# A diffusion-transformer layer on one core: everything up to LayerNorm 1 in an order from a list scheduler

## The chip, the core and the metric

The kernel runs on one core of a Trainium2 chip. Five engines work side by side, each through its own instructions in order: TensorE (PE: matmuls, and PEld its weight loads), VectorE (DVE), ScalarE (ACT), GpSimd (POOL) and SyncE (SP), which issues the DMAs of this kernel. [...] The metric is the device time of one execution in microseconds, as the median of several runs; less is better.

## The reference

One layer of a diffusion transformer in fp32: 256 latent tokens `x` and 256 context tokens `ctx`, width 2048, FFN width 5632. Cut to what matters here (the context only supplies keys and values, since there is one layer):

```python
sh1, sc1, g1, sh2, sc2, g2 = split(silu(c) @ w_ada + b_ada, 6)       # w_ada: 2048 x 12288
csh1, csc1 = the first two of split(silu(c_ctx) @ w_ada + b_ada, 6)
h  = (x   * (1 + sc1)  + sh1)  @ w_in                                # w_in: 2048 x 3072
hc = (ctx * (1 + csc1) + csh1) @ w_in
# 8 heads A: window of 128, rotary, sink logit;  8 heads B: global, q and k RMS-normalised, rotary
# each group: 2 key/value heads; latent queries see latent keys and all context keys in one softmax
heads = concat(attend_A(h, hc), attend_B(h, hc))
x = layer_norm(2**0.25 * x + g1 * (heads @ w_out))                   # LayerNorm 1; w_out: 2048 x 2048
u = x * (1 + sc2) + sh2
x = layer_norm(2**0.25 * x + g2 * ((silu(u @ w_gate) * (u @ w_up)) @ w_down))
```

## The kernel before, in words

*Products.* A product with a large weight is made to fp32 accuracy from three fast ones. A weight piece of 128 x 1024 is split into `hi` (a ScalarE copy, L121) and `lo` (VectorE: raw minus hi, L122), the tokens likewise, and `mm3` (L131 to L133) adds hi·hi, lo·hi and hi·lo in a PSUM bank. A weight load (`load_raw`, L101) brings up to 1 MB, that is four k-tiles of 512 columns, into one of six raw buffers: four in the pool `wraw` and two in `araw`, taken in the turn main, main, araw (`ring`).

*Modulation.* The columns of sh1 and sc1, for tokens and context, are sums over `w_ada` that TensorE makes in four groups of 32 columns (`ada_steps`, L230); ScalarE copies them (L237), and a small selection matmul turns them into columns (L253). g1, g2 and most of sh2 and sc2 are summed on VectorE instead (L204).

*Stages up to LayerNorm 1.* The input projection goes over groups of 1, 1, 2, 4 and 8 k-tiles (`GROUPS`). For each group `prep` makes the columns of the modulation, transposes `x` and `ctx` (L351), modulates (L355) and splits them (L357, L358); then `in_part` multiplies them with six blocks of 512 columns of `w_in` for two or four row tiles, and VectorE adds every result to its sum in SBUF (L390, L392). With the last group the attention begins: rotary and transposes of keys and queries (L435 to L461, L477), scores (four matmul lines on `wk` banks), a maximum (L499), an exponential (L507), a weighing by the inverse sum (L517), a transpose (L525), two copies into `pT` (L527), and the values (L537) for four heads at once. The output projection (`out_block`) is cut into pieces that fit between; its sums end in the residual and the statistics of LayerNorm 1 (L665 to L670, L629 to L646).

*PSUM.* Four banks `acc` for the products, three `wk` for all short work, one for the modulation's sums.

*Order.* Steps are merged by hand (`merge` spreads lists evenly over each other), and the framework's own scheduler fits instructions within that, except in the first products and around LayerNorm 1, which run as written (`manual_schedule`, L716 and L753). SP issues DMAs in the order that results, and a load waits until its raw buffer is free. Warm-up matmuls on the identity (`warm`, L707) keep TensorE busy where it would wait: 28, then 2 and 10 around the first selection, 4 before the first products, and 8 and 6 at LayerNorm 1.

*After LayerNorm 1* come gate and up (L796 on), down (L894 on) and LayerNorm 2.

Of the kernel before, what the change touches and what calls it, by code (L numbers as in the profile page):

```python
# [45 lines left out]
LAG_S = 2  # L46


@with_exitstack
def dit_layer(ctx: ExitStack, tc: tile.TileContext, x, c, cx, c_ctx, w_ada, b_ada, w_in, q_norm_g,  # L50
# [10 lines left out]
    wk_ps = ctx.enter_context(tc.tile_pool(name="wk_ps", bufs=3, space=PSUM))  # L61
# [6 lines left out]

    ada_ps = ctx.enter_context(tc.tile_pool(name="ada_ps", bufs=1, space=PSUM))
# [20 lines left out]

    ring = [wraw, wraw]
    turn = [0]

    def raw_tile():
        turn[0] += 1
        return ring[turn[0] % len(ring)].tile([P, G4 * NB], F32, tag="raw", name="raw")
# [38 lines left out]
    def rsqrt(pool, v, n, eng):  # L135
        y = pool.tile([P, n], F32, tag=f"rs_y{n}", name="rs_y", bufs=2)
        t = pool.tile([P, n], F32, tag=f"rs_t{n}", name="rs_t", bufs=2)
        nc.vector.tensor_single_scalar(t.bitcast(I32), v.bitcast(I32), 1, op=ALU.logical_shift_right)
        nc.vector.tensor_scalar(y.bitcast(I32), t.bitcast(I32), -1.0, float(0x5F3759DF), op0=ALU.mult, op1=ALU.add)
        for _ in range(3):  # L140
            eng.scalar_tensor_tensor(t, y, -0.5, y, op0=ALU.mult, op1=ALU.mult)
            eng.tensor_mul(t, t, v)
            eng.scalar_tensor_tensor(y, t, 1.5, y, op0=ALU.add, op1=ALU.mult)
        return y
# [3 lines left out]
    ring.append(ea.enter_context(tc.tile_pool(name="araw", bufs=ADA_BUFS)))  # L148
# [30 lines left out]
    def ada_vector_steps(starts, width, sums, done):  # L179


        st = {}
        ns = len(starts)
        w = ns * width
        nk = G4 * NB // w

        def step(g):
            if g == 0:
                st["a"] = sums()
                nc.gpsimd.memset(st["a"], 0.0)  # L190
                for i, c0 in enumerate(starts):
                    nc.sync.dma_start(st["a"][0:1, i * width : (i + 1) * width], b_ada[0:1, c0 : c0 + width])
            a = st["a"]
            raw = raw_tile()
            rv = raw.rearrange("p (k i n) -> p i k n", k=nk, i=ns)
            for i, c0 in enumerate(starts):
                nc.sync.dma_start(
                    rv[:, i],
                    w_ada[g * nk * P : (g + 1) * nk * P, c0 : c0 + width].rearrange("(k p) n -> p k n", p=P),
                )  # L200
            piece = min(w, 2 * NB)
            for j in range(nk):
                for c in range(0, w, piece):
                    nc.vector.scalar_tensor_tensor(a[:, c : c + piece], raw[:, j * w + c : j * w + c + piece],  # L204
                                                   cs[:, g * nk + j, 2:3], a[:, c : c + piece],
                                                   op0=ALU.mult, op1=ALU.add)
            if g == KD // nk - 1:
                done(a)

        return [lambda g=g: step(g) for g in range(KD // nk)]  # L210

# [3 lines left out]
    def ada_steps(starts, width, done, copy_tile=None):  # L215


        st = {}
        nk = G4 * NB // width
        ns = KD // nk  # L220
        nb = len(starts)

        def step(i, g):
            raw = load_raw(w_ada, g * nk, nk, starts[i], width)
            if i == 0 and g == 0:
                st["ps"] = ada_ps.tile([P, NB], F32, tag="ada", name="adaps")
            for c in range(nk):
                k = g * nk + c
                j = k % 4
                nc.tensor.matmul(  # L230
                    st["ps"][32 * j : 32 * j + 32, :width], lhsT=cs[:, k, 2 - 2 * i : 34 - 2 * i],
                    rhs=raw[:, c * width : (c + 1) * width],
                    start=(i == 0 and k < 4), stop=(i == nb - 1 and k >= KD - 4),
                )
            if i == nb - 1 and g == ns - 1:
                sb = copy_tile() if copy_tile else pa.tile([P, NB], F32, tag="t2k", name="ada", bufs=5)
                nc.scalar.copy(sb[:, :width], st["ps"][:, :width])  # L237
                done(sb)

        return [lambda i=i, g=g: step(i, g) for i in range(nb) for g in range(ns)]  # L240

    def ada_pair(c0, ncol, shift, scale, copy_tile=None, later=None):

        def done(sb):
            if later is None:
                columns(sb)
            else:
                later.append(lambda: columns(sb))

        def columns(sb):  # L250
            ps = wk_bank()
            for j in range(ncol):
                nc.tensor.matmul(ps[:, 4 * j : 4 * j + 4], lhsT=sb[:, j * P : (j + 1) * P], rhs=sel, start=True, stop=True)  # L253
            pv = ps[:, 0 : 4 * ncol].rearrange("p (j i s) -> p j i s", i=2, s=2)
            bs, bc = (bcol[:, k : k + ncol, None].to_broadcast([P, ncol, 2]) for k in (c0 // P, c0 // P + KD))
            nc.vector.tensor_tensor(shift, pv[:, :, 0, :], bs, op=ALU.add)
            nc.vector.scalar_tensor_tensor(scale, pv[:, :, 1, :], 1.0, bc, op0=ALU.add, op1=ALU.add)

        return ada_steps((c0, c0 + D), ncol * P, done, copy_tile)

    def ada_rows(c0, dst, sums):

        width = dst.shape[-1]

        def done(sb):
            for s in range(0, width, NB):
                ps = wk_bank()
                nc.tensor.matmul(ps, lhsT=ones, rhs=sb[:, s : s + NB], start=True, stop=True)  # L268
                nc.scalar.copy(dst[:, s : s + NB], ps)

        return ada_vector_steps((c0,), width, sums, done)
# [18 lines left out]
    def consts():  # L290
# [4 lines left out]
        nc.sync.dma_start(sinkb, sink_logit[0:1, :].to_broadcast([P, 8]))  # L295
        nc.gpsimd.tensor_scalar_mul(nsink, sinkb, -1.0)
        nc.vector.tensor_copy(identb, ident)
# [18 lines left out]

    qacc = [[pa.tile([P, NB], F32, tag=f"q{gi}{t}", name="qacc") for t in range(NT)] for gi in range(4)]
    u, rms, kT = {}, {}, {}
# [3 lines left out]


    kvacc = [[b4([P, 2, NB], F32, "kvacc") for _ in range(2)] for _ in range(2)]

    def prep(g):

        k0, n = GROUPS[g]
        return sum((prep_part(g, k, min(n, G4)) for k in range(k0, k0 + n, G4)), [])

    def prep_part(g, k0, n):

        st = {}

        def loads():
            nc.sync.dma_start(xt[:, :, k0 * P : (k0 + n) * P],
                              x[:, k0 * P : (k0 + n) * P].rearrange("(t p) d -> p t d", p=P))
# [640 lines left out]
```

## Time and profile before

| | us |
|---|---|
| median of 3 runs | 1190.5 (1188.59 to 1191.16) |
| the profiled execution | 1189.62 |
| its span, first to last instruction | 1187.8 |
| TensorE busy | 1158.3 (98%) |
| VectorE busy | 800.4 (67%) |
| ScalarE busy | 530.3 (45%) |
| bytes moved | 292.93 MB, mean 247 GB/s |

The page of the profile gives busy time for each engine, the granted TensorE clock (PEclk) and the DMA share in slices, the chain of waits that ended last, and groups of equal instructions with their count, busy time, mean duration, and the idle time ahead of them with what ended it. A stretch of the span can be asked for by itself (windows), and the instructions of a stretch in order of time (timeline). Matmuls are pipelined and their ends are modelled: one of 512 columns lasts 0.39 us in a row, while the next starts earlier, so starts are read here rather than durations. A fp32 matmul that is not split stands as two rows. LayerNorm 1's warm-up begins at 424.51 us of the span.

### The profile page before, as it was taken

What the parts mean: (1) busy time and instruction counts of PE and PEld (TensorE: products, weight loads), DVE (VectorE), ACT (ScalarE), POOL (GpSimd) and SP (SyncE); (2) the same over time, 40 slices, a digit from 0 to 9 for tenths busy, and PEclk for the clock granted to TensorE, in tenths of its full rate; (3) what the DMA queues carried; (4) which work ended last, traced back from release to release, by engine and by line L of the source; (5) the groups of instructions that cost most, each with busy time, mean ns of one, the idle gap of its engine ahead of it and who ended that gap; (6) DMA issues with size and microseconds to landing.
All of it is one profiled execution on the core that took longest, in us unless ns stands there. A gap on an engine that the chain in (4) does not pass through costs nothing.

```text
span 1187.8 us, 14248 instructions
## 1 busy us (share of the span) xinstructions
PE 1158.3 (98%) x5527; PEld 916.4 (77%) x5527; DVE 800.4 (67%) x1026; ACT 530.3 (45%) x762; POOL 21.1 (2%) x43
## 2 busy tenths in 40 slices
PE   8999899999999999999999999999999999999995
PEld 7666578867777768888888888888888888888884
DVE  3763289998867888775776564544545778676556
ACT  2443142668675245445544444444444434343340
POOL 1100000000000010100000000000000000000000
PEclk9999999999999999999999999999999999999997
DMA  9999878853565969998675555565565888877541
GB/s 300 375 390 375 333 272 311 297 203 108 171 214 205 309 231 348 335 314 291 212 230 177 182 196 190 180 205 183 180 208 184 313 317 318 288 256 253 200 139 71
DMA packets 150137, 292.93 MB, mean 247 GB/s; under 512 B 5515, under 2 KB 20267, under 8 KB 147765
## 3 DMA queue, kind: packets, MB, share of 16 engines
q1 hardware_dynamic: 150070, 292.03, 70.8%
q8 instruction: 43, 0.70, 0.2%
q14 instruction: 24, 0.20, 0.0%
HBM read 289.91 MB, written 2.10 MB: 246 GB/s over the span
## 4 chain that ended last, share of the span: by engine, by line
PE 92%; DVE 3%; DMA 2%; ACT 1%; SPq 1%; issue 0%; DVEq 0%; ACTq 0%
PE acc L132 27%; PE acc L133 27%; PE acc L131 27%; PE adaps L230 3%; PE wk L537 2%; DMA raw<-in_w_ada_dram 2%; PE wk L525 1%; DVE lo L122 1%; PE wk L820 1%; PE wk L131 1%; PE wk L133 1%; PE wk L132 1%; PE wk L268 1%; SPq L101 1%; DVE xt L927 0%; PE wk L602 0%
## 5 line engine op out<-in xcount | busy, mean ns | idle before, releaser
L122 DVE TENSOR_TENSOR lo<-raw,hi 128x1024 fp32r<-128x1024 f32 x344 | 415.9, 1217 | 252.1 <-ACT hi L121 247.8
L121 ACT CAST hi<-raw 128x1024 fp32r<-128x1024 f32 x344 | 358.0, 1048 | 470.5 <-PE acc L133 406.2
L131 PE MATMUL acc<-hi,u2h 128*128 128x512 f32 x704 | 275.9, 392 | 0.8 <-ACT u2h L782 0.7
L133 PE MATMUL acc<-hi,u2l 128*128 128x512 f32 x704 | 274.9, 391 | 1.3 <-DVE u2l L783 1.3
L132 PE MATMUL acc<-lo,u2h 128*128 128x512 f32 x704 | 274.7, 390 | 0.0
L133 PEld LDWEIGHTS acc<-hi,u2l 128*128 128x128 f32 x704 | 132.6, 188 | 29.3 <-DVE u2l L783 1.7
L131 PEld LDWEIGHTS acc<-hi,u2h 128*128 128x128 f32 x704 | 132.6, 188 | 28.2 <-ACT u2h L782 1.2
L132 PEld LDWEIGHTS acc<-lo,u2h 128*128 128x128 f32 x704 | 132.6, 188 | 27.0
L131 PE MATMUL acc<-hi,hTh 128*128 128x512 f32 x344 | 135.5, 394 | 0.0
L133 PE MATMUL acc<-hi,hTl 128*128 128x512 f32 x344 | 134.1, 390 | 0.0
L132 PE MATMUL acc<-lo,hTh 128*128 128x512 f32 x344 | 134.0, 390 | 0.0
L204 DVE SCALAR_TENSOR_TENSOR adav<-raw,cs,adav 128x512 f32<-128x512 f32 (+1 forms) x112 | 109.5, 977 | 13.1 <-DMA raw<-in_w_ada_dram 11.5
L132 PE MATMUL acc<-lo,uh 128*128 128x512 f32 x256 | 102.0, 399 | 2.4 <-DVE lo L122 2.4
L131 PE MATMUL acc<-hi,uh 128*128 128x512 f32 x256 | 99.5, 405 | 2.8 <-ACT hi L121 2.8
L133 PE MATMUL acc<-hi,ul 128*128 128x512 f32 x256 | 101.4, 396 | 0.0
L132 PEld LDWEIGHTS acc<-lo,hTh 128*128 128x128 f32 x344 | 64.6, 188 | 14.3 <-issue 1.0
L131 PEld LDWEIGHTS acc<-hi,hTh 128*128 128x128 f32 x344 | 64.6, 188 | 14.3 <-issue 1.0
L133 PEld LDWEIGHTS acc<-hi,hTl 128*128 128x128 f32 x344 | 64.6, 188 | 13.2
L131 PEld LDWEIGHTS acc<-hi,uh 128*128 128x128 f32 x256 | 47.5, 189 | 18.9 <-ACT hi L121 6.5
L132 PEld LDWEIGHTS acc<-lo,uh 128*128 128x128 f32 x256 | 48.6, 190 | 15.4 <-DVE lo L122 5.0
L133 PEld LDWEIGHTS acc<-hi,ul 128*128 128x128 f32 x256 | 48.6, 190 | 9.9
L131 PE MATMUL acc<-hi,oTh 128*128 128x512 f32 x128 | 50.9, 398 | 0.0
(182 smaller groups left out, 1041.8 us busy)
## 6 DMA issues: line engine op xcount, KB each, us to landing
raw<-in_w_ada_dram SPq DMA_DIRECT2D x72, 1024.0 KB, 6.9
raw<-in_w_gate_dram SPq DMA_DIRECT2D x44, 1024.0 KB, 5.0
raw<-in_w_up_dram SPq DMA_DIRECT2D x44, 1024.0 KB, 5.0
raw<-in_w_down_dram SPq DMA_DIRECT2D x44, 1024.0 KB, 5.4
raw<-in_w_ada_dram SPq DMA_DIRECT2D x48, 512.0 KB, 5.3
raw<-in_w_in_dram SPq DMA_DIRECT2D x18, 1024.0 KB, 7.5
raw<-in_w_out_dram SPq DMA_DIRECT2D x16, 1024.0 KB, 5.0
raw<-in_w_in_dram SPq DMA_DIRECT2D x4, 768.0 KB, 7.6
```

Source lines behind the costliest of these rows:

```text
L101: nc.sync.dma_start(rv.rearrange("p (k n) -> p k n", k=nk), w[k0 * P : (k0 + nk) * P, c0 : c0 + width].rearrange("(k p) n -> p k n", p=P),)
L121: nc.scalar.copy(hi[:, :n], raw[:, s : s + n])
L122: nc.vector.tensor_tensor(lo[:, :n], raw[:, s : s + n], hi[:, :n].bitcast(F32), op=ALU.subtract)
L131: nc.tensor.matmul(ps, lhsT=xh, rhs=w[0], start=first, stop=False)
L132: nc.tensor.matmul(ps, lhsT=xh, rhs=w[1], start=False, stop=False)
L133: nc.tensor.matmul(ps, lhsT=xl, rhs=w[0], start=False, stop=last)
L204: nc.vector.scalar_tensor_tensor(a[:, c : c + piece], raw[:, j * w + c : j * w + c + piece], cs[:, g * nk + j, 2:3], a[:, c : c + piece], ...
L230: nc.tensor.matmul(st["ps"][32 * j : 32 * j + 32, :width], lhsT=cs[:, k, 2 - 2 * i : 34 - 2 * i], rhs=raw[:, c * width : (c + 1) * width], ...
L268: nc.tensor.matmul(ps, lhsT=ones, rhs=sb[:, s : s + NB], start=True, stop=True)
L525: nc.tensor.transpose(t_ps[:, k * P : (k + 1) * P], pr[:, k * P : (k + 1) * P], ident)
L537: nc.tensor.matmul(o_ps, lhsT=v, rhs=pTs[t][k // 2][:, k % 2, :], start=k == 0, stop=k == 3)
L820: nc.tensor.transpose(ps[:, j * P : (j + 1) * P], hh[:, j * P : (j + 1) * P], ident)
```

## The change

From the start to LayerNorm 1 the steps are no longer merged by hand. Each piece of work is entered in a `Flow` with its engine, a cost in ns, the steps it depends on, the buffers it takes and gives back, and a due time (`F.at`). `Flow.run` goes through simulated time: whenever an engine is free it starts the ready step with the earliest due time for which buffers are free, and it finally calls the steps in that order. The whole stretch is built with `manual_schedule` for all five engines, so each engine runs in exactly this order.

With it:
- warm-ups are 56 steps of two matmuls, booked at 225 ns a step, with the latest due time of all; so they stand wherever the plan leaves TensorE empty;
- PSUM is four `acc` and four `wk` banks; the modulation's sums take a `wk` bank;
- raw buffers are named by use: the groups before the last may take any of the six, the last group, w_out and the LayerNorm 1 modulation take `wraw`, the vector sums `araw`;
- the w_in weights of the first two groups come as four loads (one, two, two and one blocks) instead of two of three blocks;
- the values are made for two heads at once (256 columns), with one copy per head into `pT`;
- output blocks are cut as (0), (0,1), (0,1), (0,1), (1), and then (2,3) four times;
- the biases of g1 and of the first sh2/sc2 sums, the identity in bf16 and the LayerNorm columns are made or loaded earlier.

From the last output block on the steps are as before.

```diff
+BLOCKS = (2, 0, 5, 1, 3, 4)
+T2K = 5
+WARM = 56
+BEGIN = 3600.0
+class Flow:
+    ENGINES = ("SP", "PE", "ACT", "DVE", "POOL")
+    SAME = {"SP": 0, "PE": 0, "ACT": 60, "DVE": 80, "POOL": 80}
+    OTHER = {"SP": 2000, "PE": 270, "ACT": 90, "DVE": 90, "POOL": 150}
+    PATIENCE = 0
...
+    def add(self, eng, ns, fn, after=(), take=(), give=(), at=None):
+        s = Step()
+        s.eng, s.ns, s.fn, s.take, s.give = eng, ns, fn, take, give
+        s.after = [a if isinstance(a, tuple) else (a, 0) for a in after if a is not None]
+        s.rank = (self.at if at is None else at, len(self.steps))
...
+    def run(self):
+        free = {e: self.begin for e in self.ENGINES}
...
+                for item in sorted(ready[e]):
+                    s = item[1]
...
+                    pools = [next((p for p in b.pools if self.room[p] > 0), None) for b in s.take]
+                    if None in pools or any(self.room[p] < pools.count(p) for p in pools):
+                        continue
...
+                    s.start, end = now, now + s.ns
+                    free[e] = end
...
+                    for n, early in s.next:
+                        n.left -= 1
+                        n.when = max(n.when, end - early + (self.SAME if n.eng == e else self.OTHER)[e])
...
+        for s in order:
+            s.fn()
...
-    wk_ps = ctx.enter_context(tc.tile_pool(name="wk_ps", bufs=3, space=PSUM))
+    wk_ps = ctx.enter_context(tc.tile_pool(name="wk_ps", bufs=4, space=PSUM))
...
-    ada_ps = ctx.enter_context(tc.tile_pool(name="ada_ps", bufs=1, space=PSUM))
...
+    region = tc.manual_schedule(engines={ET.DVE, ET.Activation, ET.PE, ET.Pool, ET.SP})
+    region.__enter__()
...
+    F = Flow({"raw": RAW_BUFS, "araw": ADA_BUFS, "hl": HL_BUFS, "acc": 4, "wk": 4, "b4": NB4, "t2k": T2K}, BEGIN)
...
+    def flow_products(hl, deps, ready, cols, ps, xs, first, last):
...
+        after = [deps[0], (deps[1], 200), ready[0], (ready[1], 400)]
+        return F.add("PE", 681 * len(cols), fn, after, [ps] if first else [], [hl])
...
-            for i in range(2):
-                nc.scalar.copy(pTs[t][i][:, :, h * P : (h + 1) * P],
-                               t_ps[:, 2 * i * P : 2 * (i + 1) * P].rearrange("p (k q) -> p k q", k=2))
...
-                nc.tensor.matmul(o_ps, lhsT=v, rhs=pTs[t][k // 2][:, k % 2, :], start=k == 0, stop=k == 3)
...
+            def gather(i, pT=pT, ps=None):
+                if i == 0:
+                    pT.t = b4([P, 4, 2, P], F32, "pT")
+                nc.scalar.copy(pT.t[:, :, i, :], ps.t.rearrange("p (k q) -> p k q", k=4))
...
+                    nc.tensor.matmul(o_ps.t[:, : 2 * P], lhsT=v, rhs=pT.t[:, k].rearrange("p h q -> p (h q)"),
+                                     start=k == 0, stop=k == 3)
...
+            s = [F.add("PE", 760, lambda i=i, f=scores: f(i), qk, [banks[i]], [*qT[gi][0], *kT[w][0]]) for i in range(2)]
+            m = [F.add("DVE", 700, lambda i=i, f=largest: f(i), [s[i]]) for i in range(2)]
+            nm = F.add("DVE", 300, bound, [*m, root])
+            e = [F.add("ACT", 760, lambda i=i, f=power: f(i), [nm], [probs[i]], [banks[i]]) for i in range(2)]
...
+            n = [F.add("ACT", 630, lambda i=i, f=weigh: f(i), [r]) for i in range(2)]
...
+            v = F.add("PE", 1800, values, g, [o_ps], [pT, *kv_room[w]])
...
+    def warm(wps, n):
         for _ in range(n):
             nc.tensor.matmul(wps, lhsT=ident, rhs=ident, start=True, stop=True)
...
     wps = acc_bank()[:, :P]
-    warm(28)
-    p = prep(0)
-    run(p[1:2])
-    run(p[:1])
-    warm(12)
...
-    run(merge(w[2:4], ks[:4], g1s[:4]))
-    run(qs[:2])
-    run(merge(attend_steps(0), w[4:6] + ks[4:] + w[6:8] + qs[2:4], g1s[4:9]))
...
+    for _ in range(WARM):
+        F.add("PE", 225, lambda: warm(wps, 2), at=1e6)
+    flow_inputs(0, (0.0, 0.0))
+    T = 18.0
...
+    for g in range(last):
+        n = GROUPS[g][1]
+        dur = 10.9 * n + 4.0 * GROUPS[g + 1][1]
...
+        span = (T + 0.1 * dur, T + 0.9 * dur) if g else (10.0, 20.0)
+        flow_inputs(g + 1, span)
+        flow_blocks(g, bs)
+        T += dur
...
+    gates = rows_of_gate(flow_vector((2 * D,), D, g1b, (gate_from, END - 15)))
...
+    F.run()
```

More of the change, by code (lines that the diff above doesn't have):

```diff
@@ L201, in step @@
[L201 to L206, printed above, removed]
+                st["a"] = first_sums(sums(), starts, width)
+            raw = raw_tile()
+            vector_load(raw, starts, width, g)
@@ L212, in vector_sums, with vector_sum @@
+    def vector_sum(raw, a, w, g, i):
+        piece = min(w, 2 * NB)
+        f = i * piece
+        j, c = f // w, f % w
+        nc.vector.scalar_tensor_tensor(a[:, c : c + piece], raw[:, f : f + piece],
+                                       cs[:, g * (G4 * NB // w) + j, 2:3], a[:, c : c + piece],
+                                       op0=ALU.mult, op1=ALU.add)
     def vector_sums(width):
         return main.tile([P, 2 * NB], F32, tag="adav", name="adav")[:, :width]
[L215 to L240, printed above, removed]
@@ L242, in ada_pair @@
-    def ada_pair(c0, ncol, shift, scale, copy_tile=None, later=None):
-        def done(sb):
[L245 to L271, printed above, removed]
+    def rows_from(sb, dst, s):
+        ps = wk_bank()
+        nc.tensor.matmul(ps, lhsT=ones, rhs=sb[:, s : s + NB], start=True, stop=True)
+        return lambda: nc.scalar.copy(dst[:, s : s + NB], ps)
@@ L846, in dit_layer @@
     z_part(0)
-    warm(6)
+    warm(wps, 6)
     z_part(2)
```

952 lines of the change are left out of this document (638 added, 314 removed).

## The prediction

> **What bounds the kernel now.** I read the page first (span, engines, chain that ended last), then the windows up to LayerNorm 1, then what TensorE waited for, then its groups by form, and last the timeline of the first 22 us.
>
> ```profile
> span 1187.8 us, 14248 instructions
> PE 1158.3 (98%) x5527; PEld 916.4 (77%) x5527; DVE 800.4 (67%) x1026; ACT 530.3 (45%) x762; POOL 21.1 (2%) x43
> ...
> PE 92%; DVE 3%; DMA 2%; ACT 1%; SPq 1%; issue 0%; DVEq 0%; ACTq 0%
> ```
>
> TensorE is the bound: 92% of the chain that ended last. The other engines matter only where they make it wait, and the change can save only such waits, since it takes no product away. The windows show where waits are visible:
>
> ```profile
> core 0: us, PE busy (x) PEld busy (x) DVE busy (x) ACT busy (x) POOL busy (x), PEclk, DMA share, GB/s
> 0.00:25.00 25.00, 19.67 (x204) 17.72 (x205) 5.99 (x11) 6.79 (x12) 4.22 (x12) 1.00 0.93 294
> 25.00:125.00 100.00, 97.76 (x580) 66.43 (x579) 59.33 (x88) 37.29 (x60) 4.69 (x13) 1.00 1.02 380
> 125.00:150.00 25.00, 21.72 (x129) 13.14 (x128) 6.47 (x9) 5.45 (x9) 0.00 (x0) 0.93 0.85 321
> 150.00:175.00 25.00, 23.62 (x103) 18.67 (x102) 20.84 (x22) 12.84 (x18) 0.00 (x0) 1.00 0.77 283
> 175.00:424.50 249.50, 249.40 (x1156) 183.31 (x1154) 214.24 (x367) 140.74 (x303) 1.50 (x4) 1.00 0.63 221
> ```
>
> Until 125 us the DMA engines are full, and TensorE visibly idles until 175; from 175 on TensorE looks full, the DMA has room, and VectorE is 86% busy. "Looks full" hides gaps, because the ends of matmuls are modelled. So I count TensorE's work from starts. The groups of 0 to 424.5 us (the warm-up matmuls ahead of LayerNorm 1's transposes start at 424.5), then rows that price one of each kind:
>
> ```profile
> L132 PE MATMUL acc<-lo,uh 128*128 128x512 f32 x256 | 102.0, 399 | 2.4 <-DVE lo L122 2.4
> L132 PE MATMUL acc<-lo,oTh 128*128 128x512 f32 x128 | 50.4, 394 | 0.0
> L132 PE MATMUL wk<-kTl,qTh 128*128 128x512 f32 x32 | 12.5, 392 | 0.0
> L230 PE MATMUL adaps<-raw,cs 128*32 128x512 f32 x256 | 32.2, 597 | 0.0
> L537 PE MATMUL wk<-pT,kvacc 128*128 128x512 f32 x64 | 29.1, 597 | 0.0
> L525 PE MATMUL wk<-ident,pr 128*128 128x128 f32 x128 | 19.0, 273 | 0.0
> ```
>
> ```profile
> 600.74 0.39 PE L131 MATMUL acc<-hi,u2h 128*128 128x512 f32 x1
> ...
> 603.46 0.39 PE L131 MATMUL acc<-hi,u2h 128*128 128x512 f32 x1
> ```
>
> ```profile
> 61.10 1.85 PE adaps L230 x16
> ...
> 244.87 0.44 PE wk L525 x4
> ...
> 260.29 3.44 PE wk L537 x8
> ```
>
> The first pair is the first and last of 13 starts: 12 matmuls in 2.72 us, 0.227 us each. An ada row costs 0.116, a transpose 0.109, a row of the values 0.43.
>
> Each of the first three groups is one of three alike (hi·hi, lo·hi, hi·lo): 3 x (256+128+32) = 1248 x 0.227 = 283.3 us. Values 64 x 0.43 = 27.5, the gate rows 8 x 0.43 = 3.4; transposes 243 (the 128 quoted and 115 of the inputs, keys and queries) x 0.109 = 26.5; ada 256 x 0.116 and, by their narrower widths, about 7.6 for the other 192 rows: 37.3; selections and masks 9.0; the two input transposes 0.7; warm-ups 12.2 (below). Together 399.9 of 424.5 us. The start:
>
> ```profile
> 0.73 0.39 SPq L153 DMA_DIRECT2D crow<-in_c_dram  x1
> 3.08 2.06 SPq L101 DMA_DIRECT2D raw<-in_w_ada_dram  x2
> 3.84 8.61 PE L707 MATMUL acc<-ident 128*128 128x128 f32 x56
> 12.37 1.96 PE L230 MATMUL adaps<-raw,cs 128*32 128x128 f32 x64
> 14.96 2.48 PE L707 MATMUL acc<-ident 128*128 128x128 f32 x20
> 17.27 0.38 PE L351 MATMUL wk<-ident,xt 128*128 128x128 f32 x2
> 21.20 1.20 PE L131 MATMUL acc<-hi,uh 128*128 128x512 f32 x4
> ```
>
> ```profile
> PE wk L158 <- DMA crow<-in_c_ctx_dram: 2.9, 1, 2.9
> PE acc L131 <- ACT hi L121: 2.8, 2, 2.1
> PE acc L132 <- DVE lo L122: 2.4, 4, 1.2
> PE adaps L230 <- DMA raw<-in_w_ada_dram: 2.0, 2, 1.5
> PE wk L253 <- ACT ada L237: 1.4, 2, 0.7
> PE wk L176 <- DMA brow<-in_b_ada_dram: 0.5, 1, 0.5
> ```
>
> Of the 24.6 us that are not work, 3.4 are the wait for the conditioning rows at the start (2.9 and 0.5, the first and the last of these waits). **21.2 us are stalls**, which is all that a better order could win up to LayerNorm 1. Most lie before 175 us; the waits are for weight pieces (hi, lo), ada weights, and the copy ahead of the selections.
>
> **The change, part by part.**
>
> *Warm-ups.* Before runs 28+2+10+4 = 44 of them, and 14 more at LayerNorm 1, which stay. Two rows are one matmul: 28 took 8.53 us (3.84 to 12.37, its first rows slow), and ten took 2.31 (14.96 to 17.27), 0.23 each. After has WARM = 56 steps of two, 112 matmuls; the planner books a step at 0.225 us where the rows give 0.46. It puts them in as the least urgent work wherever its plan leaves TensorE empty, but TensorE then runs them in order. The built order is: 56 around the four input transposes, 16 ada matmuls, 24, 16 ada, 6, the selection, 20, then the first product; 6 more before the second selection. The extra 68 x 0.23 = **+15.6 us** on the bounding engine. The first ada matmul comes at 3.84 + 8.53 + 28 x 0.23 + 4 x 0.109 = 19.3 us instead of 12.4, the first product at 19.3 + 1.96 + 50 x 0.23 + 0.3 = 33 us instead of 21.2. Some of it stands where TensorE would have waited; that is counted below as stalls not suffered.
>
> [...] The row of 125 to 150 has a granted clock of 0.93, that is 1.7 us lost, and the longest wait near it is 2.1 us (for hi). [...]
>
> *DMA order.* The first four loads fill the four main buffers. The third w_in load takes over the buffer of the first ada load, so SP cannot issue it before TensorE has used that load, at 20.3 us; the ada loads of group 1 are queued behind it, and the second of them waits for the second ada run, at about 27 us. Some 3.3 MB are moved by 13.5 us, then the DMA idles until 20. At 27 us about 5.1 MB are in, where before has 294 GB/s x 25 us = 7.4 MB and, at 380, 0.7 more: transfers run 8 us late. Up to the last ada load of group 4 the new order holds 49.8 MB, the old one 48.7, and the old one's matmuls on that load began at 143.9:
>
> ```profile
> 143.93 1.90 PE adaps L230 x16
> ```
>
> 44.7 MB more at the 0.38 MB/us of 25 to 125 us end at 145 us; at 0.35 (41.3 MB in 118.9 us, what the old order reached from 25 us to that row) they end at 155. TensorE, with no stall, reaches that load's matmuls at 150. So the wait is 0 to 5 us. I take 3.5: an ada load or a w_in load that waits for a buffer until TensorE is done with its predecessor arrives up to 1.7 us late at three places (the end of group 2, the second and fourth w_in blocks of group 3). One drop of the clock there I put at 1.0, between 0 and 1.7.
>
> *Selections.* At two places the built order still has the selections right behind the ada run whose copy they need, 0.7 us each by the wait of L253: 1.4, between 0 and 3.
>
> *SP, POOL.* Three small bias loads stand ahead of the first x and ada loads (0.4 us to issue each); TensorE comes to the ada data at 19.3 us, so they are free; without that cover 1.3 us. Tables, memsets and LayerNorm columns move within the idle of POOL (2%).
>
> *Values for two heads.* 32 matmuls of 512 columns become 64 of 256: the same columns, 27.5 us; zero, or +3 if the weight loads (0.19 us each below) no longer hide under 0.215. One ScalarE copy per head replaces two of half its size (L527), 64 rows become 32, 24.3 us at most as before; oT is made in 16 halves instead of 8 pieces, one more fixed cost each on ScalarE and VectorE. Neither is the bound: zero.
>
> ```profile
> L537 PEld LDWEIGHTS wk<-pT,kvacc 128*128 128x128 f32 x64 | 11.6, 190 | 12.6 <-issue 11.5 <-ACT pT L527 0.6 <-ACT pr L507 0.4
> L527 ACT COPY pT<-wk 128x256 f32<-128x256 f32 x64 | 20.4, 379 | 8.2 <-PE wk L525 8.1
> L517 ACT ACTIVATE pr<-pr,ll 128x512 f32<-128x512 f32 x32 | 21.4, 717 | 3.5 <-DVE ll L515 3.5
> L507 ACT ACTIVATE pr<-wk,nm,qsc 128x512 f32<-128x512 f32 x16 | 12.3, 779 | 3.6 <-DVE nm L504 3.6
> L507 ACT ACTIVATION_READ_ACCUMULATOR pr<-wk,nm,qsc 128x1 f32 x16 | 3.2, 202 | 0.0
> ```
>
> *Attention's order.* The planner books 0.63 us for the weighing and 0.76 for the exponential; the rows give 0.717, and 0.779 with an accumulator read of 0.2 behind it. For a pair of heads the probabilities come 0.4 to 0.6 us later than planned, and TensorE, which takes the transposes in planned order, waits if they were placed as soon as they were due. 16 pairs x 0.5 = 8 us if every pair pays, 0 if none does. The old order shows no such wait among its longest. I take half: 4.
>
> *One PSUM pool* (four and four banks for four, three and one), *buffers kept apart for weights and for vector sums*: no wait in the old trace names a bank; zero. The order from the last output block to the first gate products is the same, instruction for instruction: zero.
>
> **Sum.** Work 399.9 + start 3.4 + warm-ups 15.6 = 418.9 us; stalls 3.5 + 1.0 + 1.4 + 4 = 9.9. LayerNorm 1 is reached at 428.8 instead of 424.5: **+4.3 us**. The profiled execution took 1189.6 (span 1187.8), 0.9 below the median of 1190.5: 1193.9. I say 1194.
>
> **The rivals.** Everything hangs on the new stalls S: the change is S - 5.6 us. What counts as no change in this kernel is within 0.2%, 2.4 us.
>
> *Faster.* If S stays below 3.2 us the change wins. For it: TensorE starts its products 12 us later but the DMA only 8 later, so data lead by 4 us more than before; at 0.38 MB/us all ada weights are in before they are asked for. Against it: group loads still wait for six buffers, and single late pieces remain. With S = 1.5: 1185.5. The bound S = 0: 1184.
>
> *No change.* Stalls of 3.2 to 8: the warm-ups that stand in a hole cost what the holes cost, and the order buys nothing more. Centre 1190.
>
> *Attention pays in full.* All 16 pairs late (8) and the values behind their copies too (another 4): S = 18, 1202. For it: VectorE is 86% busy there, so lateness does not drain away. Against it: a stall of TensorE gives all later chains the same time back.
>
> *Stalls as before.* The new order does not do what it says: S = 21.2, only the warm-ups are added: 1205.
>
> **How the numbers follow.** Forecast (S from 8 to 14, 1192 to 1198) 0.44; attention in full or stalls as before 0.11; no change 0.18; faster 0.27. The range 1184 to 1205 spans S from 0 to 21; the likeliest case's own is 1192 to 1198.
>
> **What would show it.** The first product at 33 us (31.5 to 34.5), 224 warm-up rows before it and the next selection, DMA idle between 14 and 20 us, the last ada run of group 4 between 150 and 157; short TensorE waits for ada or w_in loads between 84 and 155 us; waits of half a microsecond on pr between 220 and 370; the LayerNorm warm-ups at about 429 us. If the first product comes at 33 and LayerNorm 1 before 422, the stalls vanished and the faster rival holds; if it comes near 21, the warm-ups cost nothing and the largest term of my sum is wrong.

## The result, and the profile after

| | before | after |
|---|---|---|
| median of 4 runs each | 1189.55 us (1186.72 to 1191.16) | 1204.32 us (1203.59 to 1206.25) |
| the profiled execution | 1189.62 us | 1205.04 us |
| its span | 1187.8 us | 1203.3 us |
| warm-ups ahead of LayerNorm 1 begin | 424.44 us | 441.05 us |

The changed kernel is slower: 1.0129 times the kernel before, 95% interval 1.0105 to 1.0154. All of it is lost up to LayerNorm 1, which is reached 16.6 us later; from the first gate product to the last product of the kernel it takes 741.2 us against 742.9.

From the page of the changed kernel, the span, the engines, and the shares of the chain that ended last:

```profile
span 1203.3 us, 14618 instructions
PE 1168.8 (97%) x5727; PEld 945.9 (79%) x5727; DVE 800.2 (67%) x1028; ACT 528.2 (44%) x738; POOL 19.0 (2%) x43
...
PE 88%; DMA 5%; DVE 5%; ACT 1%; issue 1%; SPq 0%; DVEq 0%; ACTq 0%
```

TensorE's share of the chain fell from 92 to 88%, and DMA and VectorE stand there with 5% each instead of 2 and 3. The windows up to LayerNorm 1, with the columns shown for before:

```profile
0.00:25.00 25.00, 21.89 (x218) 21.34 (x222) 3.88 (x4) 2.37 (x4) 3.48 (x9) 1.00 0.63 190
25.00:125.00 100.00, 95.25 (x636) 68.65 (x624) 55.54 (x82) 32.69 (x53) 4.95 (x16) 0.98 0.89 321
125.00:150.00 25.00, 21.89 (x125) 14.16 (x121) 7.35 (x13) 6.99 (x12) 0.00 (x0) 0.93 0.99 376
150.00:175.00 25.00, 24.24 (x131) 17.45 (x132) 17.54 (x22) 13.88 (x22) 0.00 (x0) 1.00 1.04 411
175.00:425.00 250.00, 246.85 (x1194) 199.70 (x1193) 212.86 (x352) 145.07 (x287) 0.25 (x1) 1.00 0.63 223
```

Read the last two columns first. Before, the DMA engines moved 294 GB/s up to 25 us and 380 from there to 125; now it is 190 and 321. So 7.35 + 38.0 = 45.4 MB had come by 125 us, and now 4.75 + 32.1 = 36.9: the weights run 8.5 MB behind, although the same bytes are to be moved. What TensorE waited for up to 480 us (all of them above 0.5 us):

```profile
PE acc L221 <- ACT hi L435: 4.7, 3, 2.4
PE wk L264 <- DMA crow<-in_c_ctx_dram: 2.9, 1, 2.9
PE wk L1156 <- DMA raw<-in_w_ada_dram: 2.5, 1, 2.5
PE acc L222 <- DVE lo L438: 2.3, 3, 0.8
PE wk L221 <- DVE oTl L862: 1.8, 1, 1.8
PE acc L221 <- ACT u2h L1211: 1.7, 1, 1.7
PE wk L763 <- ACT pr L822: 0.9, 1, 0.9
PE wk L472 <- DMA raw<-in_w_ada_dram: 0.9, 2, 0.6
PE wk L501 <- ACT ada L496: 0.7, 1, 0.7
```

Three late w_in pieces make the largest entry. Where they come from can be seen by laying three timelines of the changed kernel beside each other around the longest (SyncE's issues, ScalarE's casts, TensorE; in the timeline of SP a row with x2 or more spans the time from its first issue to its last, waiting included):

```profile
69.64 6.81 SPq L417 DMA_DIRECT2D raw<-in_w_ada_dram  x2
76.50 0.50 SPq L533 DMA_DIRECT2D xt<-in_x_dram  x1
77.05 0.46 SPq L538 DMA_DIRECT2D cxt<-in_ctx_dram  x1
77.61 1.11 SPq L417 DMA_DIRECT2D raw<-in_w_in_dram  x1
```

```profile
85.69 1.04 ACT L435 CAST hi<-raw 128x1024 fp32r<-128x1024 f32 x1 [13.49 <-DMA raw<-in_w_in_dram]
```

```profile
82.50 1.92 PE L472 MATMUL wk<-raw,cs 128*32 128x512 f32 x16
86.79 0.50 PE L221 MATMUL acc<-hi,uh 128*128 128x512 f32 x1 [2.36 <-ACT hi L435]
```

Of the two ada loads in the first row the second was held until 76.1 us, for a raw buffer that TensorE was still using. The two token loads and a 0.5 MB w_in load were queued behind it on SyncE and went out at 77.61. The w_in piece was there at 85.7, 8.1 us after its issue, and TensorE had stood since 84.4. At 124.7 us the same happens again (w_in issued at 118.27 behind an ada load that was held until 117.86, cast at 125.60). The waits of SyncE's queue in the first 200 us, in total, with their number and the longest, show that this is its normal state:

```profile
SPq L417 <- PE wk L472: 56.4, 17, 9.3
SPq L417 <- DVE lo L438: 43.6, 14, 8.2
```

Most of it shows as no wait of TensorE: against these 100.0 us stand 7.9 us in which TensorE waited for hi, for lo and for the ada loads of L472 in the same 200 us.

### The profile page after: what moved, and what is told of

Read it like the earlier page. It is cut to its first block, busy times and chain, and to the rows that moved or that the text cites. A ratio compares the mean times of both kernels' runs of the same rounds, so it can differ in the third digit from the quotient of the medians.

```text
span 1203.3 us, 14618 instructions
## 1 busy us (share of the span) xinstructions
PE 1168.8 (97%) x5727; PEld 945.9 (79%) x5727; DVE 800.2 (67%) x1028; ACT 528.2 (44%) x738; POOL 19.0 (2%) x43
## 4 chain that ended last, share of the span: by engine, by line
PE 88%; DMA 5%; DVE 5%; ACT 1%; issue 1%; SPq 0%; DVEq 0%; ACTq 0%
PE acc L221 26%; PE acc L222 26%; PE acc L223 26%; DMA raw<-in_w_ada_dram 3%; PE acc L1032 2%; DMA raw<-in_w_in_dram 2%; PE wk L472 2%; PE wk L851 2%; DVE adav L326 1%; PE wk L1249 1%; PE wk L840 1%; DVE lo L438 1%; PE wk L221 0%; PE wk L1156 0%; DVE xt L1356 0%
## 5 line engine op out<-in xcount | busy, mean ns | idle before, releaser
L212 DVE TENSOR_TENSOR lo<-raw,hi 128x1024 fp32r<-128x1024 f32 x262 | 318.1, 1223 | 229.2 <-ACT hi L211 225.6
L211 ACT CAST hi<-raw 128x1024 fp32r<-128x1024 f32 x262 | 274.9, 1054 | 348.3 <-PE acc L223 319.7
L435 ACT CAST hi<-raw 128x1024 fp32r<-128x1024 f32 (+1 forms) x82 | 83.9, 1031 | 143.8 <-DMA raw<-in_w_in_dram 70.4
L438 DVE TENSOR_TENSOR lo<-raw,hi 128x1024 fp32r<-128x1024 f32 (+1 forms) x82 | 97.1, 1194 | 42.3 <-ACT hi L435 42.2
L221 PE MATMUL acc<-hi,uh 128*128 128x512 f32 x256 | 104.1, 407 | 4.8 <-ACT hi L435 4.7
```

The lines of the kernel that those rows point to most:

```text
L211: nc.scalar.copy(hi[:, :n], raw[:, s : s + n])
L212: nc.vector.tensor_tensor(lo[:, :n], raw[:, s : s + n], hi[:, :n].bitcast(F32), op=ALU.subtract)
L221: nc.tensor.matmul(ps, lhsT=xh, rhs=w[0], start=first, stop=False)
L435: nc.scalar.copy(hl.hi[:, :n], raw.t[:, s : s + n])
L438: nc.vector.tensor_tensor(hl.lo[:, :n], raw.t[:, s : s + n], hl.hi[:, :n].bitcast(F32), op=ALU.subtract)
```

## The experiments

All times are medians with the range; the ratio is to the kernel before, measured on the same chip. The runs come from several chips, so two runs that do not stand on the same chip are compared more safely by their ratios (e1 to e4 share one chip, e5 to e8 one, e9 to e11 one).

| run | us | ratio, 95% interval |
|---|---|---|
| e1_one_warm | 1195.89 (1193.62 to 1196.09) | 1.0063 (1.0048 to 1.0078) |
| e2_no_warm | 1194.75 (1194.08 to 1195.05) | 1.0057 (1.0042 to 1.0072) |
| e3_before_more_warm | 1200.29 (1199.87 to 1201.75) | 1.0106 (1.0089 to 1.0123) |
| e4_m1_early | 1211.14 (1209.40 to 1212.98) | 1.0196 (1.0180 to 1.0211) |
| e5_one_warm_own_buffers | 1199.40 (1197.86 to 1202.07) | 1.0099 (1.0082 to 1.0115) |
| e6_own_buffers | 1211.65 (1208.28 to 1213.64) | 1.0205 (1.0188 to 1.0222) |
| e7_own_buffers_ln1_loads | 1191.39 (1189.82 to 1202.12) | 1.0041 (1.0017 to 1.0064) |
| e8_own_buffers_no_warm | 1190.33 (1188.23 to 1191.57) | 1.0019 (1.0010 to 1.0028) |
| e9_buffers_in_step | 1188.60 (1184.51 to 1190.76) | 0.9995 (0.9984 to 1.0006) |
| e10_loads_ahead | 1183.13 (1181.77 to 1184.49) | 0.9951 (0.9939 to 0.9963) |
| e11_two_warm_in_step | 1202.71 (1198.74 to 1205.57) | 1.0114 (1.0092 to 1.0136) |
| e12_loads_ahead_alone | 1185.83 (1183.62 to 1187.43) | 0.9981 (0.9972 to 0.9990) |

### How much of the warm-ups lies on the path

Three kernels: the changed one with half of its planned warm-ups, with none, and the old one with 68 more.

```diff
-        F.add("PE", 225, lambda: warm(wps, 2), at=1e6)
+        F.add("PE", 225, lambda: warm(wps, 1), at=1e6)
```

> The changed kernel with one warm-up matmul in each of the 56 steps instead of two, so that a step lasts what the planner books; the order of all else is the same. Theory A (the surplus warm-ups stand on TensorE's path): 56 x 0.22 = 12.3 us less than the changed kernel's 1204.3, so 1192, with the same 22 us of stalls. Theory B (the supply of weights is the bound, the warm-ups only fill waits): the waits at the ends of groups 2 and 3 grow by what the warm-ups no longer fill, 1200 to 1204.

```diff
-WARM = 56
+WARM = 0
```

> The changed kernel without any of the 112 warm-up matmuls up to LayerNorm 1, all else in the same order. Theory A: 25 us less but for 2 us of slow clock at the first products, so about 1181. Theory B: the first product comes early, at about 20 us, but later waits for ada and w_in loads take it back; not under 1195.

```diff
-    warm(28)
+    warm(96)
```

> The kernel before with the 68 extra warm-up matmuls at its start (96 instead of 28), its own order otherwise. Theory A: 68 x 0.23 = 15.6 us slower, 1205. Theory B: less than half of that, 1191 to 1197, because the stalls between 100 and 160 us shrink while the DMA runs ahead as far as six buffers allow.

In the old order 68 extra warm-ups cost 1200.3 - 1188.0 = 12.3 us of the 15.6 that they last: four fifths are on the path. In the new order the first 56 that are taken away save 8.4 us of 12.9 (7.8 by the ratios), but the other 56 only 1.1, and there the ranges overlap. Without them TensorE waits in their place, as its timeline in the kernel with no planned warm-ups shows:

```profile
6.97 0.69 PE L558 MATMUL wk<-ident,xt 128*128 128x128 f32 x2 [3.15 <-DMA xt<-in_x_dram]
...
11.56 1.93 PE L472 MATMUL wk<-raw,cs 128*32 128x128 f32 x32 [3.30 <-DMA raw<-in_w_ada_dram]
15.18 1.93 PE L472 MATMUL wk<-raw,cs 128*32 128x128 f32 x32 [1.69 <-DMA raw<-in_w_ada_dram]
...
19.75 0.79 PE L221 MATMUL acc<-hi,uh 128*128 128x512 f32 x1 [1.67 <-ACT uh L571]
```

With one matmul per step the first product comes at 20.45 us, with none at 19.75. Slow first products, as in theory A, are there: with none they start 0.43 us apart from 20.34 to 21.62 us, with one per step 0.23 apart from 20.79 on. A slow clock is not shown; the granted clock of 0 to 25 us reads 1.00 in both. So the half that the plan books fills holes that are there; the half that it does not book (a step of two lasts 0.46 us, booked as 0.225) is about two thirds loss. And the warm-ups are half of the story only: without any the new order is still 6.8 us slower than the old one, with 88 warm-up rows fewer. Neither theory was right alone.

### LayerNorm 1: the load or the matmuls

TensorE waited 2.5 us for the last ada load (L1156 above), and its granted clock is 0.84 from 440 to 450 us. The first attempt had the last five loads due 32 us earlier and allowed them into the buffers of the vector sums too, while the due time of their matmuls stayed:

```diff
+            F.at = END + (12 + 8 * g if i == 0 and g < 3 else 28)
+            raw, ld = flow_load(w_ada, g * 4, 4, (3 + i) * D + NB, NB, W if i == 0 and g < 3 else ("araw", "raw"))
             F.at = END + (12 + 8 * g if i == 0 and g < 3 else 60)
-            raw, ld = flow_load(w_ada, g * 4, 4, (3 + i) * D + NB, NB, W)
```

> The changed kernel, with the last five ada loads of the LayerNorm 1 modulation due 32 us earlier and allowed into the vector-sum buffers; their matmuls keep their due time. The 2.5 us wait of the last ada matmuls on their DMA, and the clock drop and waits right behind it, go: 3 to 4.5 us less, 1200 to 1201. If those waits lie beside the LayerNorm chain of VectorE, which ends later, nothing changes: 1204.

It was 7 us slower than the changed kernel, which neither expectation had. The wait for the load is gone. But a step that is ready is started ahead of its due time when its engine has nothing more urgent, so the scheduler also took the matmuls earlier, the last one ahead of the last output products. LayerNorm 1 begins no earlier (441.11 us instead of 441.05), and behind it the chain of LayerNorm 1 on VectorE lost its cover:

```profile
PE wk L1206 <- DVE xt L970: 4.6, 1, 4.6
```

### Which buffer a load gets

The scheduler counts free buffers; the framework chooses which of them a tile gets. In the built program of the changed kernel (and of the one with one warm-up, whose plan is the same) two of 112 loads, planned at 61.98 and 99.62 us, were given a buffer that the plan has in use for 3.2 and 3.1 us more, while another was free. They are the two loads behind which the w_in loads of 77.61 and 118.27 us stand. (The w_out loads, too, may take any of the six buffers in the code, unlike what the list of the change says; four of them take one of the two in `araw`.) The next kernels give each raw buffer a tag of its own, which the scheduler names; behind LayerNorm 1, where this scheduler does not plan, the four main ones are taken in plain turn:

```diff
-    F = Flow({"raw": RAW_BUFS, "araw": ADA_BUFS, "hl": HL_BUFS, "acc": 4, "wk": 4, "b4": NB4, "t2k": T2K}, BEGIN)
+    F = Flow({**{p: 1 for p in MAIN + SIDE}, "hl": HL_BUFS, "acc": 4, "wk": 4, "b4": NB4, "t2k": T2K}, BEGIN)
...
+    def raw_tag():
+        turn[0] += 1
+        return f"raw{turn[0] % RAW_BUFS}"
...
-            room.t = pools[room.pool].tile([P, G4 * NB], F32, tag="raw", name="raw")[:, : nk * width]
+            room.t = pools[room.pool].tile([P, G4 * NB], F32, tag=room.pool, name="raw")[:, : nk * width]
```

> One warm-up per step as in the run that took 1195.9 us; in addition each of the six raw buffers has a name of its own, in the plan and in the program. In the program of that earlier run two loads (the 25th and the 38th of the weights, planned at 61.98 and 99.62 us) were given a buffer that the plan has in use for 3.2 and 3.1 us more, while another buffer was free; SyncE stood there for 6.0 and 9.4 us, and TensorE waited for the w_in pieces behind them at 72.65 and 114.5 us. Theory R (the buffer that is handed out is the cause of these two waits): the lag behind the plan, which jumps by 4.9 us at each of the two places, does not jump, 9.8 us are saved, and the time is 1185 to 1188. Rival L (the pieces are late because several loads share the DMA engines, 8 us from issue to landing where the plan books 2 beyond the transfer): the waits stay or move by a few us, 1192 to 1196.

> The changed kernel with its two warm-ups per step, and each raw buffer with a name of its own. Theory R: the two jumps of the lag behind the plan, 4.2 us at the wait of 83.8 us and 3.9 at the wait of 124.7, are gone, and the time is 1195 to 1198; of the 16 us by which the changed kernel is later at LayerNorm 1, half is then due to the two buffers and half to the warm-ups. Rival L: 1201 to 1205.

Both came out slower, by 3.5 and 7.3 us than the same kernels without the tags, above every range expected, and the traces say why: LayerNorm 1 was reached earlier (426.7 instead of 430.3, and 434.2 instead of 441.1), but behind it the buffers were now taken in plain turn. The stretch from the first gate product to the last product took 747.5 and 747.0 us instead of 742.4 and 741.2, and right behind LayerNorm 1 stood a wait that is 1.7 us long in the kernels without the tags (here with one warm-up):

```profile
PE acc L229 <- ACT u2h L1219: 4.9, 2, 4.5
```

So these two say something up to LayerNorm 1 only: the second of the two w_in waits is gone, the first remains (2.0 and 2.2 us). The next kernel asks for the last ada loads earlier, by 24 us instead of 32, with which TensorE's matmuls stay behind the last output products; one more leaves out the warm-ups; and two have, behind LayerNorm 1, the changed kernel's own sequence of buffers again.

```diff
-            raw, ld = flow_load(w_ada, g * 4, 4, (3 + i) * D + NB, NB, W)
+            due, late = F.at, i > 0 or g == 3
+            F.at = END + 36 if late else due
+            raw, ld = flow_load(w_ada, g * 4, 4, (3 + i) * D + NB, NB, MAIN + SIDE if late else W)
+            F.at = due
```

> One warm-up per step, own buffers, and the last five ada loads of LayerNorm 1 asked for earlier (due 36 us after the end of the attention instead of 60, and allowed in all six buffers), while TensorE takes their matmuls at the same place, behind the last output products. If the 3.0 us wait for the last of these loads is on the path: 3 us less than the kernel without it, that is 1182 to 1185 by theory R. If the chain of LayerNorm 1 on VectorE takes its place, as it did in the run in which the matmuls came earlier: within 1 us of the kernel without it.

> As the kernel with own buffers and earlier LayerNorm 1 loads, without the warm-up steps. In the changed order the last 56 warm-ups cost 1.1 us. If they still only fill holes in which TensorE waits for the first loads: 1 to 2 us less than the kernel with one warm-up per step. If the clock needs them: 1 to 4 us more.

> As the run with own buffers, one warm-up per step and earlier LayerNorm 1 loads (1191.4 us), which reaches LayerNorm 1 at 421.96 us (the kernel before: 424.44) but then takes 745.6 us from the first gate product to the last product where the changed kernel takes 741.2. There the buffers were handed out in plain turn after LayerNorm 1. Here they are handed out in the sequence of the changed kernel again. If that turn is the cause: 741 to 743 us behind LayerNorm 1 and 1186 to 1189 in all. If something else makes the rest longer: 1190 to 1192.

> The changed kernel, two warm-ups per step, with own buffers up to LayerNorm 1 and its own sequence of buffers behind. In the earlier run with plain turn LayerNorm 1 was reached at 434.2 us instead of 441.1. If the two loads with the wrong buffer are worth those 6.8 us and nothing else changes: 1196 to 1199. If the gain is lost again at LayerNorm 1: 1202 to 1205.

The earlier ada loads took 8.0 us off (1199.4 to 1191.4), more than their 3: the 4.9 us wait above fell to 1.9 with them, and the two can't be told apart here. With and without warm-ups the times are 1191.4 and 1190.3 with ranges that overlap: nothing can be said. With the sequence restored the rest takes 741.0 and 742.2 us again, so plain turn was its cause, and the kernel with one warm-up, own buffers and earlier LayerNorm 1 loads is level with the kernel before. But in the changed kernel with its two warm-ups the own buffers bring 1202.7, which is 1.6 us instead of the 5 to 8 expected: the other expectation, 1202 to 1205, came out. It reached LayerNorm 1 at 437.7 us, where the kernel with two warm-ups and plain turn, which is the same up to there, had 434.2. In these two traces the granted clock from 25 to 125 us was 0.97 and 1.00, and 0.03 of 100 us is 3 us, so a few us at LayerNorm 1 between two single traces can come from one execution's clock. Own buffers alone are a small part, and theory R falls for the first of the two waits: it stays in every one of these runs. Its load goes out at 66.07 us with buffers in step, and went out at 66.42 with one warm-up alone.

### Loads asked for earlier

The scheduler gives a load the due time of its own products, and books 2 us from the end of the transfer to the first use. Two numbers give it room:

```diff
-    OTHER = {"SP": 2000, "PE": 270, "ACT": 90, "DVE": 90, "POOL": 150}
+    OTHER = {"SP": 3000, "PE": 270, "ACT": 90, "DVE": 90, "POOL": 150}
...
+        due = F.at
+        F.at = due - 6
         raw, ld = flow_load(w, k0, nk, c0, width, where)
+        F.at = due
```

> As the run with buffers in step, and the plan books 3 us instead of 2 from the end of a transfer to its use and asks for the w_in and w_out loads 6 us earlier than for their products. Theory L for what is left of the front's waits (2.1 and 1.0 us at 74 us, 1.1 and 1.0 at 133, 1.0 at 46: pieces that land later than planned): they shrink, 3 to 6 us less than the run with buffers in step, 1181 to 1185. Rival: the earlier loads take buffers from the ada loads, whose waits grow by as much, within 2 us of that run.

> The changed kernel with one warm-up per step and the loads planned ahead (3 us instead of 2 from the end of a transfer to its use, w_in and w_out loads asked for 6 us before their products), without names for the buffers and without the earlier LayerNorm 1 loads. In this plan no load is given a buffer that the plan has in use. Theory L (late pieces are the front's waits, and the buffers only add to it): as the run with all three, 1183.1 us, plus the 3 us of the LayerNorm 1 wait, that is 1185 to 1188, 8 to 11 less than with one warm-up per step alone. If the own buffers are what took the second wait away: 1190 to 1194.

Both came out as expected: 5.5 us less than the kernel with buffers in step, and, on top of the changed kernel with one warm-up and nothing else, a ratio of 0.9981 instead of 1.0063, that is 0.0082 x 1189 = 9.8 us. In this second plan no load is given a buffer that is in use, without any tags. Other steps move with the loads: TensorE takes some of its steps in another order too, and what that is worth by itself was not tried. Its window of 25 to 125 us, and all that TensorE waited for between 60 and 160 us:

```profile
25.00:125.00 100.00, 96.31 (x598) 66.57 (x600) 58.88 (x84) 31.23 (x47) 4.94 (x16) 1.00 1.02 378
```

```profile
PE acc L222 <- DVE lo L441: 1.5, 2, 0.8
PE wk L504 <- ACT ada L499: 0.8, 1, 0.8
PE acc L221 <- ACT hi L438: 0.4, 1, 0.4
```

The DMA engines are full again (378 GB/s where the changed kernel had 321 and one warm-up alone 348), the wait for hi fell to 0.4 us (4.7 in the changed kernel, 5.7 with one warm-up alone), and the clock stays at 1.00. How far TensorE is behind the time that the scheduler itself planned for it shows the same in one line per kernel (the plan of the first two is the same; in the third each step has its own):

| TensorE behind its plan, us | ada run before the first w_in wait | after it | end of group 4 | middle of the attention | last ada run of LayerNorm 1 |
|---|---|---|---|---|---|
| changed kernel | 12.1 | 16.3 | 18.7 | 18.3 | 20.6 |
| with one warm-up | 0.9 | 5.8 | 9.5 | 9.2 | 10.6 |
| with one warm-up and loads ahead | 0.7 | 2.1 | 0.8 | -0.3 | -1.8 |

The first column is the price of the unbooked warm-ups, and the next steps are the late w_in pieces. From there to the last column, through the whole attention, the first kernel loses 1.9 us more, the second 1.1, and the third gains about 2.5. The 1183.1 us of the kernel with all edits (one warm-up, loads ahead, own buffers, earlier LayerNorm 1 loads) beat both kernels, by 0.5% and 1.8%; with two edits, the warm-up and the loads, it is 1185.8.

## Why the prediction was right or wrong

The direction was right, the time was not the likeliest one: 1204.3 is at the upper end of the range, well above the 1192 to 1198 of the forecast, where the rival "stalls as before" stood with 1205. That the range holds it is luck rather than insight, since it runs from no stalls at all to as many as before. The rival's sum is met, but not its picture: the old order with as many warm-ups takes 1200.3 us, and of the new order's stalls, listed below, those of the attention and of the last ada load were not there before.

*Warm-ups: right, as a term.* The first product came at 31.55 us (33 predicted, 31.5 to 34.5 allowed), and the rows are there:

```profile
L1032 PE MATMUL acc<-ident 128*128 128x128 f32 x224 | 27.8, 285 | 0.0
```

```profile
31.55 0.48 PE L221 MATMUL acc<-hi,uh 128*128 128x512 f32 x1
```

The experiments put the part that is on the path at 12.3 of 15.6 us in the old order, and at 8.4 of 12.9 in the new one for the half that the plan does not book; the prediction counted the rest as stalls not suffered, and that is where it went.

*The idle DMA: right, but it begins 2 us later than said.* From 14 to 16 us the engines still move 324 GB/s, and then next to nothing until 20:

```profile
16.00:18.00 2.00, 2.00 (x22) 1.88 (x25) 0.69 (x1) 0.16 (x1) 0.00 (x0) 1.00 0.01 4
18.00:20.00 2.00, 2.00 (x41) 1.80 (x42) 0.00 (x0) 0.00 (x0) 0.00 (x0) 1.00 0.00 0
```

*Stalls: 9.9 said, about 22 there.* LayerNorm 1 at 441.05 less 418.9 leaves 22.2. Where TensorE stands longer than its form does in a row (an ada run of 16 rows takes 1.85 us up to the next start when nothing waits), the excess adds up to 20.4 with the clock; the other 2 us are not placed (418.9 is itself an estimate). The 20.4 go to the terms of the sum like this:

| term | said (bounds) | trace | what it was |
|---|---|---|---|
| DMA order | 3.5 (0 to 5) | 9.4 | w_in pieces at 83.8, 124.7 and 148.8 us (3.5, 2.5, 2.1), ada loads at 47.4 and 55.8 (1.3) |
| clock | 1.0 (0 to 1.7) | 3.4 | two drops, 0.17 x 10 us each (below) |
| selections | 1.4 (0 to 3) | 0.8 | one, at 93.7 us |
| attention's order | 4 (0 to 8) | 3.7 | three waits, at 289.6, 362.9 and 379.3 us |
| last output block to LayerNorm 1 | 0 | 3.1 | the last ada load, at 436.4 us |

*The step that failed* is the DMA's: 3.5 us in the sum, 9.4 in the trace, beyond the bound of 5. From 27 us on it took the engines at 0.35 to 0.38 MB/us, what the old order reaches, and concluded that the last ada load of group 4 is reached between 150 and 157 us. The engines reached 0.321:

```profile
164.26 1.92 PE L472 MATMUL wk<-raw,cs 128*32 128x512 f32 x16
```

The bounds had a waiting load arrive up to 1.7 us late at three places, for itself. What was missed is the queue: SyncE issues in order, so a load that waits for a buffer holds all loads behind it, here for up to 9.3 us (the longest of the waits of L417 above), and the engines run low meanwhile (187 GB/s from 70 to 77 us, 275 from 108 to 118). The prediction saw this at the third w_in load at the start and did not follow it further. Asking for the loads earlier took the wait for hi away and filled the engines again, with the same bytes to move; so it is shown that the plan's order, with the loads where it put them, is the cause and not the bandwidth. How much of it is the queue behind the waiting load, and how much only that the load was asked for too late, no run separates.

The booking is part of it. The plan books 1.05 MB / 390 + 2 = 4.7 us for a 1 MB load. The page of the changed kernel has, as the medians from issue to landing,

```profile
raw<-in_w_in_dram SPq DMA_DIRECT2D x18, 1024.0 KB, 7.9
raw<-in_w_out_dram SPq DMA_DIRECT2D x16, 1024.0 KB, 4.9
```

so the booking holds for w_out, in a stage where the DMA is 63% busy, and not for w_in, whose loads go out among the ada loads, up to 231 us, with a DMA share of 0.89, 0.99 and 1.04 in the windows from 25 to 175 us. The two loads with the wrong buffer are another part, worth 1.6 us by the run with two warm-ups, whose range is wide.

*The clock: right in kind, undercounted.* The waits for hi of 2.36 and 1.38 us are each followed by one matmul and a second wait, for lo, of 0.8 us; so from 84.42 to 88.05 us and from 125.31 to 127.96 TensorE made a single matmul. A lower clock follows both, in the windows of the changed kernel:

```profile
85.00:95.00 10.00, 6.75 (x29) 3.74 (x29) 3.82 (x4) 2.73 (x4) 0.00 (x0) 0.83 1.05 404
125.00:135.00 10.00, 7.85 (x29) 5.85 (x26) 2.96 (x3) 1.99 (x2) 0.00 (x0) 0.83 1.05 407
```

0.17 of 10 us is 1.7 us each: more than half of what the waits took came on top. The prediction allowed for one drop, up to the 1.7 us of the one in the old trace; here two came, the second behind a stretch of 2.65 us. In the kernel without warm-ups the same pair of waits, 1.43 and 0.77 us around one matmul, in 2.69 us from 116.19 us on, left the clock at 1.00, so it isn't each wait.

```profile
115.00:125.00 10.00, 7.81 (x40) 5.40 (x33) 2.96 (x3) 1.99 (x2) 0.00 (x0) 1.00 1.05 409
```

*Attention: the size right, the cause wrong.* No series of half-microsecond waits on pr came. TensorE keeps its distance to the plan through 16 pairs, so the booked costs of the exponential and the weighing are good enough. The prediction added up durations; from start to start two exponentials with the read between them are 0.67 us apart, less than the 0.76 booked, as ScalarE's timeline has it:

```profile
289.88 0.69 ACT L822 ACTIVATE pr<-wk,nm 128x512 f32<-128x512 f32 x1 [0.84 <-PE wk L803]
290.46 0.19 ACT L822 ACTIVATION_READ_ACCUMULATOR pr<-wk,nm 128x1 f32 x1
290.55 0.68 ACT L822 ACTIVATE pr<-wk,nm 128x512 f32<-128x512 f32 x1
```

The wait at 289.6 us is for a PSUM bank (L763 waits for L822 in the list: the scores of two pairs hold all four wk banks, and the transposes of the queries need one), which contradicts the zero given to the one PSUM pool. The one at 362.9 is again a load. On VectorE, in its timeline:

```profile
362.18 1.28 DVE L326 SCALAR_TENSOR_TENSOR adav<-raw,cs,adav 128x1024 f32<-128x1024 f32 x1 [1.64 <-DMA raw<-in_w_ada_dram]
363.38 1.22 DVE L438 TENSOR_TENSOR lo<-raw,hi 128x1024 fp32r<-128x1024 f32 x1
364.52 0.42 DVE L862 TENSOR_TENSOR oTl<-wk,oTh 128x256 fp32r<-128x256 f32 x1
```

A vector sum waits for its load, and the subtraction that would free a bank stands behind it.

*The values: right.* 128 rows at 0.216 us from start to start, 25.8 us in all against 26.2.

*LayerNorm 1: wrong.* "The same, instruction for instruction" is true of TensorE's order and says nothing of when a load lands. The last ada load was due last of all and confined to four buffers:

```profile
433.32 3.64 PE L1156 MATMUL wk<-raw,cs 128*32 128x512 f32 x32
439.42 1.70 PE L1156 MATMUL wk<-raw,cs 128*32 128x512 f32 x8 [2.46 <-DMA raw<-in_w_ada_dram]
441.05 1.22 PE L1032 MATMUL acc<-ident 128*128 128x128 f32 x4
```

In the kernel with all edits this wait is gone, and its whole time is 2.7 us below the one with two edits (3.6 by the ratios, as they stand on different chips); but own buffers are part of that difference too.

## What to carry to other kernels

When a plan orders loads, book them with room: a load that was asked for just in time stood here behind every load that waited for a buffer, and one such wait (the two ada loads at 69.64 us, 6.8 us from the first issue to the last) was paid by the whole DMA (187 GB/s from 70 to 77 us) and then by the clock (0.83 from 85 to 95 us). To cost a new order, follow the queue that issues the loads instruction by instruction, with the buffer that each one waits for, rather than taking the old order's bandwidth for granted. And compare the chip with the plan's own times first: the places where the distance jumps are the list of what to mend.

## What was not expected of the hardware

TensorE's granted clock dropped behind stretches of 3.6 and 2.7 us with a single matmul in each (0.83 over ten us), each time for about 1.7 us of lost work, and not behind another of 2.7 us (1.00 over ten us), in the same program region of another run. Filler matmuls in front of the first products cost 65% of their length in the new order (the half that the plan does not book) and 79% in the old, although TensorE waits for data in part of that time without them (9.8 us in the four waits of the listing with none). Two per step also hold up the DMA, since the ada matmuls that free raw buffers come later (the first two runs of them at 17.92 and 24.49 us, with none at 11.56 and 15.18): 190 GB/s in the first 25 us, against 249 with one per step and 234 with none.
